# The state-space part of a decoder trunk: its two large matrices in quarters that share five small rooms

## The chip, the cores and the metric

The kernel runs on one core of a Trainium2 chip. The metric is the device time of one execution in microseconds (us). A core has five engines with an instruction queue each, worked off in order: TensorE (PE in the profile; its weight loads PEld), VectorE (DVE), ScalarE (ACT), GpSimd (POOL) and SyncE (SP), which here only issues DMAs. They meet through semaphores.

## The reference, cut to what matters

The program is a trunk of two residual layers on 512 tokens of width 1024 (an even layer, a routed expert block, an odd layer, a routed expert block). The change lies in the odd layer, whose mixer is attention (four heads; projections for keys, queries and values) beside a state-space layer "S5":

```python
def s5_mixer(u, ...):            # 32 groups of 16 channels, each one 64-dim complex diagonal state
    lam_bar = exp(lam * step)
    b_bar = ((lam_bar - 1) / lam) * b
    bu = einsum('gpc,btgc->btgp', b_bar, u)
    states = associative_scan(x_t = lam_bar * x_{t-1} + bu_t)
    y = einsum('gcp,btgp->btgc', c_mat, states).real + d_skip * u
    z = gelu(y)
    return z * sigmoid(z @ w_glu)
```

## The kernel before, in words

The 512 tokens of S5 are cut into 64 blocks of eight. Inside a block the output is one matrix product with the block's own inputs (a Toeplitz matrix, as the answer depends on the distance of two tokens alone); from block to block a state is carried by a scan. The generator `states()` does it in these steps:

- **Input map.** For two parts r (real, imaginary) and four quarters q of the groups, POOL and DVE build W, PE transposes it and ACT copies it into `Wt` (L1976 to L1990). `Wt` is one tile of 32x128 numbers on 128 partitions in the room `s5_wm`, which exists once.
- **Toeplitz kernel.** PE multiplies B by powers of the transition (`pk`, L2002), ACT copies the product to `Ks`, DVE adds the skip term, and POOL issues four DMAs of `Ks` to `Kd` in HBM (L2017).
- **States.** For two halves q of the groups PE computes `pj` from `Wt` and the inputs `U` (L2031); DVE and POOL rotate, scan and rotate back (L2037 to L2051) and leave the states in `XP`, first part r = 0, then r = 1.
- **Toeplitz form.** `M` (L2053) is again 32x128 numbers on 128 partitions and takes the same single room `s5_wm`. Eight DMAs (L2057) on SP's queue read `Kd` with overlapping rows.
- **Output.** For four quarters PE sums `M` times `U` (L2063) and Q times `XP` (L2067) in `pyy`, and ACT copies each quarter to z (L2070), which lies in the memory of the rotation's tables cs and sn (`s_csn`). Of these 48 matmuls of a quarter, 16 read `M`.

Beside `states()` runs `to_attention()`: projections (L1883 to L1885, three matmuls for each product, called `pu`) for keys, queries and values. Each takes its weights from a ring of three rooms that SP fills in the plan's order, in four pairs of 128 rows; ACT and DVE split a pair into `whi` (L160) and `wlo` (L161), and 24 matmuls use it. After keys and queries come a norm, rotary (`us`, `wk`: L1930, L1932, L1936) and transposes (`ptq`, L1941). `run_all` interleaves both generators step by step when the program is written; after that a scheduler in the compiler layer orders every engine's queue. The stage ends with the last `pu` of the values; attention and the GLU gate follow (`pzt`, L2203, is the first transpose of z). The weights of the GLU and of the output projection come over SP's queue behind those of `to_attention()`.

Of the kernel before, what the change touches and what calls it, by code (L numbers as in the profile page):

```python
# [8 lines left out]
F32 = mybir.dt.float32  # L9
# [3 lines left out]
AF = mybir.ActivationFunctionType  # L13
OP = mybir.AluOpType
# [1765 lines left out]
def odd_mixer(K, I, x, dbg):  # L1780
    tc, nc = K.tc, K.nc
    V, G, A = nc.vector, nc.gpsimd, nc.scalar
    ident = K.ident
    H = (slice(0, 64), slice(64, 128))
# [7 lines left out]
    def bank(name):  # L1792
        return ps.tile([128, 512], F32, name=name, tag="ps", bufs=4)
# [13 lines left out]
    Kd = dram.tile([32, 16, 240], F32, name="Kd")  # L1807
# [9 lines left out]
    for k in range(KD):  # L1817
        p = bank("pt")
# [145 lines left out]
    def flat_w(name, a, b):  # L1964
        return st.tile([128, 512], F32, name=name, tag="s5_w", bufs=4).rearrange("p (a b) -> p a b", a=a)

    def states():

        Bb = [S.B[:, r, :, None, :].to_broadcast([128, 16, 8, 16]) for r in range(2)]
        P7 = []  # L1970
        for r in range(2):
            p7 = st.tile([128, 16, 8], F32, name=f"s5_p7{r}", bufs=1)
            for s in range(8):
                G.tensor_copy(p7[:, :, s], S.L[:, r, :, 7 - s])
            P7.append(p7[:, :, :, None].to_broadcast([128, 16, 8, 16]))
        Wt = st.tile([128, 32, 128], F32, name="s5_Wt", tag="s5_wm", bufs=1)  # L1976
        Wt = Wt.rearrange("p (r i) n -> p r i n", r=2)
        for r in range(2):
            for q in range(4):
                sl = slice(4 * q, 4 * q + 4)  # L1980
                W = flat_w("s5_W", 4, 128).rearrange("p i (s c) -> p i s c", s=8)
                t8 = flat_w("s5_t8", 4, 128).rearrange("p i (s c) -> p i s c", s=8)
                G.tensor_tensor(W, Bb[0][:, sl], P7[r][:, sl], OP.mult)
                V.tensor_tensor(t8, Bb[1][:, sl], P7[1 - r][:, sl], OP.mult)
                V.tensor_tensor(W, W, t8, OP.add if r else OP.subtract)
                yield
                p = bank("pw").rearrange("p (a n) -> p a n", a=4)
                for a in range(4):
                    nc.tensor.transpose(p[:, a, :], W[:, a].rearrange("p s c -> p (s c)"), ident)
                A.activation(Wt[:, r, sl, :], p, AF.Copy)  # L1990

        Ks = st.tile([128, 2, 4, 128], F32, name="s5_Ks", tag="s5_xp", bufs=1)
        G.memset(Ks, 0.0)
        zt = st.tile([16, 112], F32, name="s5_zt", bufs=1)
        G.memset(zt, 0.0)
        G.dma_start(Kd.rearrange("g c n -> c g n")[:, :, 0:112], zt[:, None, :].to_broadcast([16, 32, 112]))
        for h in range(2):
            p = bank("pk").rearrange("p (a n) -> p a n", a=4)
            for i in range(16):
                a, cg = divmod(i, 4)  # L2000
                for r in range(2):
                    nc.tensor.matmul(p[32 * cg:32 * cg + 16, a, :], S.B[H[h], r, i, :],  # L2002
                                     S.Q[r][H[h], i, 0:8, :].rearrange("p j c -> p (j c)"),
                                     start=r == 0, stop=r == 1, tile_position=(64 * h, 32 * cg))
                if i == 7:
                    yield
            for cg in range(4):
                A.activation(Ks[32 * cg:32 * cg + 16, h], p[32 * cg:32 * cg + 16], AF.Copy)
            yield
        td = st.tile([128, 8, 16], F32, name="s5_td", bufs=1)  # L2010
        V.tensor_tensor(td, i16[:, None, :].to_broadcast([128, 8, 16]),
                        dsk[:, :, None].to_broadcast([128, 8, 16]), OP.mult)
        k0 = Ks.rearrange("p h a n -> p (h a) n")[:, :, 0:16]
        V.tensor_tensor(k0, k0, td, OP.add)
        for cg in range(4):
            dst = Kd.rearrange("(ha q) c n -> c ha q n", q=4)[:, :, cg, 112:240]
            G.dma_start(dst, Ks[32 * cg:32 * cg + 16].rearrange("p h a n -> p (h a) n"))  # L2017
        yield

        XP = st.tile([128, 2, 16, 65], F32, name="s5_XP", tag="s5_xp", bufs=1)  # L2020
        G.memset(XP[:, :, :, 0], 0.0)
        for q in range(2):
            X = [flat_w("s5_X", 8, 64) for r in range(2)]
            Y = [flat_w("s5_Y", 8, 64) for r in range(2)]
            pj = []
            for r in range(2):
                p = bank(f"pj{r}").rearrange("p (i k) -> p i k", i=8)
                for a in range(8):
                    i = 8 * q + a
                    for h in range(2):  # L2030
                        nc.tensor.matmul(p[H[h], a, :], Wt[:, r, i, 64 * h:64 * h + 64],  # L2031
                                         U[:, 16 * h + i, :], start=True, stop=True)
                pj.append(p)
                yield
            sl = slice(8 * q, 8 * q + 8)
            c, s = S.cs[:, sl], S.sn[:, sl]
            V.tensor_tensor(X[0], pj[0], c, OP.mult)  # L2037
            V.tensor_tensor(Y[0], pj[1], s, OP.mult)
            G.tensor_tensor(X[0], X[0], Y[0], OP.add)
            V.tensor_tensor(X[1], pj[1], c, OP.mult)  # L2040
            V.tensor_tensor(Y[1], pj[0], s, OP.mult)
            G.tensor_tensor(X[1], X[1], Y[1], OP.subtract)
            yield
            for r in range(2):
                V.tensor_tensor_scan(fl(Y[r]), fl(S.rho[:, sl]), fl(X[r]), 0.0, op0=OP.mult, op1=OP.add)
            yield
            X = [flat_w("s5_X", 8, 64) for r in range(2)]
            for r in range(2):
                V.tensor_tensor(X[0], Y[r], c, OP.mult)
                G.tensor_tensor(X[1], Y[1 - r], s, OP.mult)  # L2050
                V.tensor_tensor(XP[:, r, sl, 1:65], X[0], X[1], OP.add if r else OP.subtract)  # L2051
                yield
        M = st.tile([128, 32, 128], F32, name="s5_M", tag="s5_wm", bufs=1)  # L2053
        for s in range(8):
            src = bass.AP(tensor=Kd.tensor, offset=Kd.offset + (7 - s) * 16,
                          ap=[[240, 16], [3840, 32], [1, 128]])
            nc.sync.dma_start(M[16 * s:16 * s + 16], src)  # L2057
        for q in range(4):
            p = bank("pyy").rearrange("p (a n) -> p a n", a=4)
            for a in range(4):  # L2060
                i = 4 * q + a
                for h in range(2):
                    nc.tensor.matmul(p[H[h], a, :], U[:, 16 * h + i, :], M[:, 16 * h + i, :],  # L2063
                                     start=True, stop=False)
                for r in range(2):
                    for h in range(2):
                        nc.tensor.matmul(p[H[h], a, :], XP[H[h], r, i, 0:64],  # L2067
                                         S.Q[r][H[h], i, 1:9, :].rearrange("p j c -> p (j c)"),
                                         start=False, stop=r == 1)
            A.activation(z[:, :, 4 * q:4 * q + 4, :].rearrange("p t i c -> p i t c"),  # L2070
                         p.rearrange("p a (t c) -> p a t c", t=8), AF.Copy)
            yield
# [3 lines left out]
    st = tc.alloc_tile_pool(name="odd_st", bufs=1, side="right")  # L2076
    U = st.tile([128, 32, 64], F32, name="s5_U")
    todo = states()
    run_all((to_states(), 9), (part(todo, SN), SN))
    run_all((to_attention(), 30), (todo, 24))  # L2080
# [342 lines left out]
```

## Time and profile before

| | us |
|---|---|
| median of three runs | 1644.34 (1642.44 to 1648.06) |
| profiled execution, whole | 1643.12 |
| its span from first to last instruction | 1641.4 |
| PE busy in the span | 1528.8 (93%) |
| DVE, ACT, POOL busy | 819.5, 447.9, 230.4 |
| odd layer's projections and S5, first `pu` to first `pzt` | 872.30 to 1020.97 |

Times in the trace count from the span's start. In a timeline row, the first number is the start, the second the duration; a bracket is the idle time of the engine before it and what ended it. Matmuls overlap: one of 512 columns lasts 0.39 us at full clock, and the next starts 0.23 us after it.

### The profile page before, as it was taken

How to read it: one execution, taken by the hardware profiler on the slowest of the kernel's cores; microseconds unless marked ns; L12 is line 12 of the kernel's file. 1: busy time of each engine (PE TensorE's matmuls, PEld its weight loads, DVE VectorE, ACT ScalarE, POOL GpSimd, SP SyncE). 2: the span in 40 equal slices, each digit the busy share in tenths (PEclk: the TensorE clock that was granted, in tenths of full speed). 3: DMA queues.
4: the chain of work that ended last, by engine and by line, in shares of the span. 5: the costliest groups of instructions: out<-in, count | busy, mean ns of one | idle time of the engine just before them, and what ended most of it. 6: DMA issues, size and time to landing. Idle time of an engine off the chain costs nothing. (4 is left out here: it accounts for less than half of the span.)

```text
span 1641.4 us, 24906 instructions
## 1 busy us (share of the span) xinstructions
PE 1528.8 (93%) x9852; PEld 886.1 (54%) x9852; DVE 819.5 (50%) x1942; ACT 447.9 (27%) x1029; POOL 230.4 (14%) x268
## 2 busy tenths in 40 slices
PE   8998988999999999999998998799999999999997
PEld 6776666776444444433348775577544444433433
DVE  5577878776233333332764694764433333322323
ACT  5234434332212121111314533741021211211110
POOL 2342331200000000000211242501000000000000
PEclk9999999999999999999999999799999999999999
DMA  7210100177899999999992262209789999999996
GB/s 223 97 65 21 51 4 2 53 295 294 337 420 419 419 420 420 420 419 418 420 387 63 66 94 59 103 26 356 308 363 420 419 420 420 419 420 421 420 420 236
DMA packets 95564, 453.62 MB, mean 276 GB/s; under 512 B 12507, under 2 KB 30715, under 8 KB 49360
## 3 DMA queue, kind: packets, MB, share of 16 engines
q1 hardware_dynamic: 88144, 438.01, 67.9%
q0 software_dynamic: 5968, 13.58, 2.4%
q8 instruction: 80, 1.31, 0.3%
q10 hardware_dynamic: 1328, 0.36, 0.1%
q14 instruction: 44, 0.36, 0.1%
HBM read 452.91 MB, written 6.78 MB: 280 GB/s over the span
## 5 line engine op out<-in xcount | busy, mean ns | idle before, releaser
L1198 PE MATMUL pgu<-w,XT 128*64 128x512 f32 x1920 | 452.4, 596 | 22.3 <-DMA w<-in_moe_w_gate 19.1
L1198 PEld LDWEIGHTS pgu<-w,XT 128*64 128x64 f32 x1920 | 141.9, 137 | 312.3 <-issue 256.6
L1288 DVE TENSOR_TENSOR x<-pc,x 128x512 f32<-128x512 f32 x240 | 149.3, 682 | 163.6 <-PE pc L1198 163.6
L1198 PE MATMUL pd<-w,hTe 128*64 128x512 f32 x960 | 213.9, 598 | 0.6 <-ACT hTe L1336 0.6
L1327 DVE SCALAR_TENSOR_TENSOR hid<-hid,gs,pgu 128x512 f32<-128x512 f32 x32 | 23.9, 747 | 242.6 <-PE pgu L1198 234.9
L1095 POOL DMA_INDIRECT rows<-rows,idx x30 | 30.0, 999 | 759.6 <-DVE O L1215 590.3
L1198 PEld LDWEIGHTS pd<-w,hTe 128*64 128x64 f32 x960 | 66.6, 137 | 122.7 <-issue 112.9
L1256 ACT ACTIVATE XT<-pga,p_norm 128x128 f32<-128x128 f32 x240 | 68.3, 371 | 195.1 <-PE pga L1198 191.3
L1345 DVE TENSOR_TENSOR ylo<-pd,yhi 128x512 fp32r<-128x512 f32 (+1 forms) x68 | 44.8, 659 | 138.8 <-ACT yhi L1344 138.8
L1326 ACT ACTIVATE hid<-pgu,gs 128x512 f32<-128x512 f32 x32 | 22.0, 688 | 288.9 <-PE pgu L1198 288.9
L1198 PE MATMUL pc<-yhi,S 128*128 128x512 f32 x240 | 100.4, 418 | 0.0
L1198 PE MATMUL pc<-ylo,S 128*128 128x512 f32 x240 | 94.9, 395 | 0.0
L1344 ACT ACTIVATE yhi<-pd 128x512 fp32r<-128x512 f32 (+1 forms) x68 | 38.9, 572 | 170.9 <-PE pd L1198 153.4
L161 DVE SCALAR_TENSOR_TENSOR wlo<-w,p_norm,whi 128x512 fp32r<-128x512 f32 (+1 forms) x72 | 56.3, 813 | 44.9 <-ACT whi L160 44.9
L160 ACT ACTIVATE whi<-w,p_norm 128x512 fp32r<-128x512 f32 (+1 forms) x72 | 46.3, 692 | 77.8 <-PE pu L665 42.3
L1198 PEld LDWEIGHTS pc<-yhi,S 128*128 128x128 f32 x240 | 45.3, 189 | 34.1 <-issue 26.0
L664 PE MATMUL pu<-hhi,whi 128*128 128x512 f32 x144 | 58.6, 411 | 0.2 <-DVE u L672 0.2
L665 PE MATMUL pu<-hlo,whi 128*128 128x512 f32 x144 | 57.8, 401 | 0.0
L1884 PE MATMUL pu<-wlo,hhi 128*128 128x512 f32 x128 | 53.4, 419 | 3.4 <-DVE wlo L161 3.4
L666 PE MATMUL pu<-hhi,wlo 128*128 128x512 f32 x144 | 55.2, 402 | 0.0
L1883 PE MATMUL pu<-whi,hhi 128*128 128x512 f32 x128 | 51.0, 416 | 1.7 <-ACT us L1895 1.7
L1885 PE MATMUL pu<-whi,hlo 128*128 128x512 f32 x128 | 52.5, 416 | 0.0
(539 smaller groups left out, 2502.7 us busy)
## 6 DMA issues: line engine op xcount, KB each, us to landing
w<-in_moe_w_down SPq DMA_DIRECT2D x120, 1024.0 KB, 20.0
w<-in_moe_w_gate SPq DMA_DIRECT2D x120, 1024.0 KB, 20.0
w<-in_moe_w_up SPq DMA_DIRECT2D x120, 1024.0 KB, 20.2
w<-in_even_w_in SPq DMA_DIRECT2D x8, 1024.0 KB, 5.2
w<-in_moe_w_gate SPq DMA_DIRECT2D x16, 512.0 KB, 8.2
w<-in_moe_w_up SPq DMA_DIRECT2D x16, 512.0 KB, 9.6
w<-in_moe_w_down SPq DMA_DIRECT2D x16, 512.0 KB, 9.3
w<-in_odd_w_in SPq DMA_DIRECT2D x8, 1024.0 KB, 5.1
```

Source lines behind the costliest of these rows:

```text
L160: nc.scalar.activation(hi[:, k, :], w[:, k, :], AF.Copy, scale=g[:, k:k + 1])
L161: nc.vector.scalar_tensor_tensor(lo[:, k, :], w[:, k, :], g[:, k:k + 1], r32(hi[:, k, :]), op0=OP.mult, op1=OP.subtract)
L664: nc.tensor.matmul(out[j], a, hhi[:, kt, :], start=kt == 0, stop=False)
L665: nc.tensor.matmul(out[j], a, hlo[:, kt, :], start=False, stop=False)
L666: nc.tensor.matmul(out[j], b, hhi[:, kt, :], start=False, stop=kt == KD - 1)
L1198: return self.K.tc.keep_in_program_order(op(*args, **kw))
L1256: nc.scalar.activation(self.XTs[j][:, k, :], p[:, i, :], AF.Copy, scale=B.gain[:, k:k + 1])
L1288: V.tensor_tensor(self.x[:, t, c], p, self.x[:, t, c], OP.add)
L1345: self.nc.vector.tensor_tensor(yl[:, c], p, r32(yh[:, c]), OP.subtract)
L1883: nc.tensor.matmul(out[j], a, whi[:, k, :], start=kt == 0, stop=False)
L1884: nc.tensor.matmul(out[j], a, wlo[:, k, :], start=False, stop=False)
L1885: nc.tensor.matmul(out[j], b, whi[:, k, :], start=False, stop=kt == KD - 1)
```

## The change

`Wt` becomes four tiles of a quarter's size and `M` four others; all eight take turns in a room `s5_wm` that exists five times. The loop over Wt runs quarter by quarter. The fifth room is free from the start, so `M0` can be loaded as soon as `Kd` is written; M1 and M2 take the rooms of Wt0 and Wt1, which the first half of `pj` reads last, and M3 that of Wt2, which the second half reads last. `Ks` and `Kd` are laid out by quarters, so that a quarter of `M` is eight consecutive rows of groups. Each quarter is loaded by eight DMAs of 64 KB, where `M` was loaded by eight of 256 KB. The rooms take 20 KB of each partition, where they took 16 KB. The skip term is added in two operations of half the size.

```diff
-        Wt = st.tile([128, 32, 128], F32, name="s5_Wt", tag="s5_wm", bufs=1)
-        Wt = Wt.rearrange("p (r i) n -> p r i n", r=2)
-        for r in range(2):
-            for q in range(4):
+        Wt = [st.tile([128, 2, 4, 128], F32, name=f"s5_Wt{q}", tag="s5_wm", bufs=5) for q in range(4)]
+        for q in range(4):
+            for r in range(2):
...
-                A.activation(Wt[:, r, sl, :], p, AF.Copy)
+                A.activation(Wt[q][:, r], p, AF.Copy)
...
-        k0 = Ks.rearrange("p h a n -> p (h a) n")[:, :, 0:16]
-        V.tensor_tensor(k0, k0, td, OP.add)
+        for h in range(2):
+            k0 = Ks[:, :, h, 0:16]
+            V.tensor_tensor(k0, k0, td[:, 4 * h:4 * h + 4], OP.add)
...
+        M = []
+        def toeplitz(n):
+            for q in range(len(M), len(M) + n):
+                M.append(st.tile([128, 2, 4, 128], F32, name=f"s5_M{q}", tag="s5_wm", bufs=5))
+                for s in range(8):
+                    src = bass.AP(tensor=Kd.tensor, offset=Kd.offset + 8 * q * 3840 + (7 - s) * 16,
+                                  ap=[[240, 16], [3840, 8], [1, 128]])
+                    nc.sync.dma_start(M[q][16 * s:16 * s + 16].rearrange("p h a n -> p (h a) n"), src)
+        toeplitz(1)
...
         for q in range(2):
...
+            toeplitz(2 - q)
...
-        M = st.tile([128, 32, 128], F32, name="s5_M", tag="s5_wm", bufs=1)
-        for s in range(8):
-            src = bass.AP(tensor=Kd.tensor, offset=Kd.offset + (7 - s) * 16,
-                          ap=[[240, 16], [3840, 32], [1, 128]])
-            nc.sync.dma_start(M[16 * s:16 * s + 16], src)
...
-                    nc.tensor.matmul(p[H[h], a, :], U[:, 16 * h + i, :], M[:, 16 * h + i, :],
+                    nc.tensor.matmul(p[H[h], a, :], U[:, 16 * h + i, :], M[q][:, h, a, :],
```

The scheduler lays out the queues anew. In the rows below, lines of the changed kernel are 9 to 15 higher from the output on: its L2029 is the load of `M`, L2044 `pj`, L2072 and L2076 are the two products of `pyy`, L2079 is the copy to z.

On SP, the weights of S5 and of the projections, before:

```order
L1491 DMA w_8297<-in_odd_w_in 128x4x512
L1491 DMA w_8580<-in_s5_w_glu 128x4x512
L2057 DMA s5_M_8418<-Kd_7397 16x32x128 x8
L1491 DMA w_8642<-in_odd_w_out 128x2x1024
L1491 DMA w_8735<-in_odd_w_out 128x2x1024
```

and of the change (w_8297 and w_8328 are the second half of the values' weights):

```order
L1491 DMA w_8328<-in_odd_w_in 128x4x512
L2029 DMA s5_M0_8096<-Kd_7397 16x8x128 x8
L1491 DMA w_8611<-in_s5_w_glu 128x4x512
L2029 DMA s5_M1_8164<-Kd_7397 16x8x128 x8
L2029 DMA s5_M2_8173<-Kd_7397 16x8x128 x8
L2029 DMA s5_M3_8360<-Kd_7397 16x8x128 x8
L1491 DMA w_8673<-in_odd_w_out 128x2x1024
L1491 DMA w_8766<-in_odd_w_out 128x2x1024
```

The first quarter moved ahead of the GLU's weights, and the three others follow them.

On PE, at the first quarter of `pyy`, before (pu3_8579 is the last accumulator of the values in their second pair of weights, wlo_8613):

```order
L1884 MATMUL pu3_8579<-wlo_8613,hhi_7400 128x512
L1885 MATMUL pu3_8579<-whi_8612,hlo_7401 128x512
L2063 MATMUL pyy_8427<-s5_M_8418,s5_U_7525 64x128 x2
L2067 MATMUL pyy_8427<-s5_Q0_6601,s5_XP_8092 64x128 x2
L2067 MATMUL pyy_8427<-s5_Q1_6602,s5_XP_8092 64x128 x2
```

and of the change (pu3_8227 is the last accumulator of the queries, pu0_8607 the first of the values):

```order
L2044 MATMUL pj1_8311<-s5_U_7525,s5_Wt3_7581 64x64 x8
L1883 MATMUL pu3_8227<-whi_8375,hhi_7400 128x512
L1884 MATMUL pu3_8227<-wlo_8376,hhi_7400 128x512
L1885 MATMUL pu3_8227<-whi_8375,hlo_7401 128x512
L1883 MATMUL pu3_8227<-whi_8375,hhi_7400 128x512
L1884 MATMUL pu3_8227<-wlo_8376,hhi_7400 128x512
L1885 MATMUL pu3_8227<-whi_8375,hlo_7401 128x512
L2072 MATMUL pyy_8458<-s5_M0_8096,s5_U_7525 64x128 x2
L2076 MATMUL pyy_8458<-s5_Q0_6601,s5_XP_8105 64x128 x2
L1883 MATMUL pu0_8607<-whi_8613,hhi_7400 128x512
```

The first quarter's matmuls stand 45 products of the values further ahead, right behind the queries; 10 products of the values stand between its first four matmuls and the rest.

On ACT, around the first copy to z, before (whi_8612, whi_8644 and whi_8674 are the values' second, third and fourth pair):

```order
L160 ACTIVATE whi_8612<-w_8197,p_norm_84 128x512 x2
L1917 ACTIVATE sq_8385<-us3_8370 128x512
L160 ACTIVATE whi_8644<-w_8297,p_norm_84 128x512 x2
L2070 ACTIVATE s5_csn_6600<-pyy_8427 128x4x8x16
L160 ACTIVATE whi_8674<-w_8297,p_norm_84 128x512 x2
```

and of the change (whi_8643, whi_8675 and whi_8705 are the same three pairs):

```order
L160 ACTIVATE whi_8643<-w_8228,p_norm_84 128x512 x2
L1917 ACTIVATE sq_8425<-us3_8410 128x512
L2079 ACTIVATE s5_csn_6600<-pyy_8458 128x4x8x16
L160 ACTIVATE whi_8675<-w_8328,p_norm_84 128x512 x2
L160 ACTIVATE whi_8705<-w_8328,p_norm_84 128x512 x2
```

The copy to z moved ahead of the third pair's split. It overwrites the tables that DVE and POOL still read for the second half of the states (L2049 and L2050 of before), so it waits for those, and both splits wait behind it. On DVE, `wlo` of the third pair moved behind the last XP, and `wk` of the first token block ahead of `wlo` of the fourth pair.

## Rows read from the trace of the kernel before

**Rows 1.** Page, part 2: GB/s in 40 slices of the span.

```profile
GB/s 223 97 65 21 51 4 2 53 295 294 337 420 419 419 420 420 420 419 418 420 387 63 66 94 59 103 26 356 308 363 420 419 420 420 419 420 421 420 420 236
```

**Rows 2.** Tile s_M: duration ns min/median/max, first and last start; who waited; landing.

```profile
L2057 SPq DMA_DIRECT2D s_M<-Kd x8: 340/569/2412, 967.3 to 973.8; - x8
...
  PE pyy L2063: 4.4, 1
...
DMA to landing us min/median/max: 4.8/11.7/15.7
```

**Rows 3.** DMA view of 966 to 992 us: GB/s in 40 slices of 0.65 us.

```profile
GB/s 25 0 0 80 242 105 91 98 120 96 92 116 111 95 93 123 104 96 93 128 100 92 98 127 97 95 95 132 95 94 98 128 128 112 101 365 403 403 195 0
```

**Rows 4.** Timeline of PE around the load of M (start, us, engine, line, tiles).

```profile
965.13 2.08 PE L2031 MATMUL pj<-s_U,s_Wt 128*64 128x64 f32 x64
...
974.22 1.09 PE L1883 MATMUL pu<-whi,hhi 128*128 128x512 f32 x4
978.68 0.80 PE L1884 MATMUL pu<-wlo,hhi 128*128 128x512 f32 x1 [3.37 <-DVE wlo L161]
...
989.71 0.69 PE L2063 MATMUL pyy<-s_M,s_U 128*64 128x128 f32 x4 [4.37 <-issue]
...
995.50 0.51 PE L1883 MATMUL pu<-whi,hhi 128*128 128x512 f32 x1
...
1003.02 0.60 PE L1941 MATMUL ptq<-idt,wk 128*128 128x128 f32 x4
...
1016.43 0.48 PE L1883 MATMUL pu<-whi,hhi 128*128 128x512 f32 x1
...
1020.97 1.04 PE L2203 MATMUL pzt<-idt,s_csn 128*128 128x128 f32 x8
```

**Rows 5.** Stretches: PE, PEld, DVE, ACT, POOL busy (count), granted clock, DMA share, GB/s.

```profile
902.30:905.30 3.00, 3.00 (x8) 2.34 (x7) 2.34 (x1) 0.37 (x1) 3.00 (x9) 0.50 0.97 311
...
978.70:984.00 5.30, 5.30 (x13) 4.15 (x14) 5.20 (x10) 0.00 (x0) 1.75 (x2) 0.50 1.29 107
989.70:994.50 4.80, 4.79 (x36) 3.02 (x36) 4.62 (x6) 0.00 (x0) 3.22 (x2) 0.52 0.28 112
```

**Rows 6.** Timeline of PE: the idle time ahead of the first of these stretches.

```profile
900.99 0.50 PE L1883 MATMUL pu<-whi,hhi 128*128 128x512 f32 x1 [1.66 <-ACT us L1895]
```

**Rows 7.** Timeline of POOL: the stores of Kd, and the last product of the states.

```profile
943.85 2.14 POOL L2017 DMA_DIRECT2D Kd<-s_Ks  x4 [21.36 <-DVE rst L138]
...
983.52 1.84 POOL L2050 TENSOR_TENSOR s_X<-s_Y,s_csn 128x512 f32<-128x512 f32 x1 [1.14 <-DVE s_XP L2051]
```

**Rows 8.** DMA issues of 880 to 1010 us: KB each, median us to landing.

```profile
Kd<-s_Ks POOLq DMA_DIRECT2D x4, 64.0 KB, 2.5
```

**Rows 9.** Timeline of SP: the GLU's weights.

```profile
956.75 0.37 SPq L1491 DMA_DIRECT2D w<-in_s_w_glu  x1
```

**Rows 10.** Timeline of DVE: states, and the queries' rotary.

```profile
969.11 0.68 DVE L2051 TENSOR_TENSOR s_XP<-s_X 128x512 f32<-128x512 f32 x1
...
973.03 0.68 DVE L2051 TENSOR_TENSOR s_XP<-s_X 128x512 f32<-128x512 f32 x1
...
989.02 4.63 DVE L1930 TENSOR_TENSOR us<-us,rsq 128x512 f32<-128x512 f32 x4
993.57 0.75 DVE L1934 TENSOR_TENSOR sq<-us,ts 128x256 f32<-128x256 f32 x2
997.32 0.75 DVE L161 SCALAR_TENSOR_TENSOR wlo<-w,p_norm,whi 128x512 fp32r<-128x512 f32 x1 [3.00 <-ACT whi L160]
997.99 0.68 DVE L1936 TENSOR_TENSOR wk<-wk,sq 128x512 f32<-128x512 f32 x1
```

**Rows 11.** Timeline of ACT: the third pair's split, and the first copy to z.

```profile
974.42 1.34 ACT L160 ACTIVATE whi<-w,p_norm 128x512 fp32r<-128x512 f32 x2 [2.18 <-PE pu L1885]
995.67 0.60 ACT L2070 ACTIVATE s_csn<-pyy 128x512 f32<-128x512 f32 x1 [19.91 <-PE pyy L2067]
```

**Rows 12.** Waits of SP's queue, 1040 to 1160 us: total, times, longest.

```profile
SPq L1491 <- PE po L2251: 23.7, 1, 23.7
```

More of the change, by code (lines that the diff above doesn't have):

```diff
@@ L1989, in states @@
                     nc.tensor.transpose(p[:, a, :], W[:, a].rearrange("p s c -> p (s c)"), ident)
-                A.activation(Wt[:, r, sl, :], p, AF.Copy)
-        Ks = st.tile([128, 2, 4, 128], F32, name="s5_Ks", tag="s5_xp", bufs=1)
+                A.activation(Wt[q][:, r], p, AF.Copy)
+        Ks = st.tile([128, 4, 2, 128], F32, name="s5_Ks", tag="s5_xp", bufs=1)
         G.memset(Ks, 0.0)
@@ L2007, in states @@
             for cg in range(4):
-                A.activation(Ks[32 * cg:32 * cg + 16, h], p[32 * cg:32 * cg + 16], AF.Copy)
+                A.activation(Ks[32 * cg:32 * cg + 16, :, h], p[32 * cg:32 * cg + 16], AF.Copy)
             yield
@@ L2012, in states @@
                         dsk[:, :, None].to_broadcast([128, 8, 16]), OP.mult)
-        k0 = Ks.rearrange("p h a n -> p (h a) n")[:, :, 0:16]
-        V.tensor_tensor(k0, k0, td, OP.add)
+        for h in range(2):
+            k0 = Ks[:, :, h, 0:16]
+            V.tensor_tensor(k0, k0, td[:, 4 * h:4 * h + 4], OP.add)
         for cg in range(4):
             dst = Kd.rearrange("(ha q) c n -> c ha q n", q=4)[:, :, cg, 112:240]
-            G.dma_start(dst, Ks[32 * cg:32 * cg + 16].rearrange("p h a n -> p (h a) n"))
+            G.dma_start(dst, Ks[32 * cg:32 * cg + 16].rearrange("p a h n -> p (a h) n"))
         yield
+        M = []
[7 more added lines that the diff above has]
+        toeplitz(1)
         XP = st.tile([128, 2, 16, 65], F32, name="s5_XP", tag="s5_xp", bufs=1)
@@ L2030, in states @@
                     for h in range(2):
-                        nc.tensor.matmul(p[H[h], a, :], Wt[:, r, i, 64 * h:64 * h + 64],
+                        nc.tensor.matmul(p[H[h], a, :], Wt[i // 4][:, r, i % 4, 64 * h:64 * h + 64],
                                          U[:, 16 * h + i, :], start=True, stop=True)
```

## The prediction

> **What bounds the kernel now.** I read the page's GB/s line first. From about 1230 us (31st of 40 slices of 41 us) to the end the DMA engines move 420 GB/s in nearly every slice [rows 1]: there the stream of the experts' weights is the bound, so a change in the odd layer counts only if it makes that stream start earlier. The waits of SP's queue say that it does: SP stands 23.7 us for PE's output projection of the attention [rows 12]. That projection hangs on one chain from the odd layer's projections, on which PE is nearly always busy. So I carry a shift of the first `pzt` (1020.97, [rows 4]) one to one to the end.
>
> Next, PE's timeline around the load of `M`. PE stands 3.37 us for `wlo` at 978.68 and 4.37 us ahead of the first `pyy` at 989.71 [rows 4]; the tile view gives that second wait to `M` [rows 2]. After each, the table of stretches shows the lower clock level (1.2 GHz, 0.50 and 0.52) for 5.3 and 4.8 us [rows 5]. In the first, 13 matmuls start in 5.3 us, 0.41 each; at 2.4 GHz 20 of them start between 1016.43 and 1020.97, 0.227 each [rows 4]. A slow microsecond thus loses 1 - 0.227/0.41 = 0.45 us: 5.3 lose 2.4, 4.8 lose 2.1. The whole loss is 3.37 + 4.37 + 2.4 + 2.1 = 12.2 us.
>
> **The load of M.** `M` waits for the end of `pj` at 967.2 (965.13 + 2.08, [rows 4]); eight DMAs leave from 967.3 to 973.8 and land 4.8 to 15.7 us later [rows 2], the last near 989.5. Meanwhile the DMA engines move about 100 GB/s [rows 3], 0.26 MB each, 2.1 MB in all.
>
> After: POOL issues the stores of `Kd` from 943.85 for 2.14 us [rows 7], the last lands 2.5 us later [rows 8]: 948.5. Then `M0` goes out, 8 x 0.57 (the issue of [rows 2]) = 4.6 us, and its 0.52 MB take 5.2 us at 100 GB/s: it lands by 958. It stands ahead of the GLU's weights, which left at 956.75 [rows 9]; the eight issues end at 953, so they cost those nothing. M1 waits for the first half of `pj`, about 957, and M3 for the second, 967.2. The three have 1.57 MB, 15.7 us at 100 GB/s, and 1 MB of the GLU stands among them: all land by about 976. That is if 64 KB pieces flow as 256 KB pieces did; the rows of `Kd` read are as short as before. The added 24 issues are 24 x 0.57 = 13.7 us of SP's time, behind which only the output projection's weights stand, not urgent. The skip term's second operation adds some 0.3 us on DVE long before its reader: nothing.
>
> On such small pieces a rule speaks against the change. The row says that a 64 KB store takes 2.5 us from issue to landing [rows 8] and that eight loads fly at once [rows 2, 3]. The Trainium skill, "DMA: Bandwidth & Descriptors", section "Rules for kernel authors", says that many small transfers should be merged, since at such sizes most is overhead; its section "Anatomy of one DMA" gives about 2.0 us fixed plus bytes by 436 GB/s. One behind the other that is an estimate of 2.15 x 24 = 52 us for M1 to M3, and would cost PE about 5 us at the last quarter; overlapped it costs nothing. The next part goes by the rows; the serial case is a rival below.
>
> **What PE then waits for.** The order puts the first quarter's products 45 products of the values further ahead, so other waits come up.
>
> - `pj` ends 967.2, six `pu` follow to 968.6, M0's products, then PE needs XP of r = 0: 969.11 + 0.68 = 969.8 [rows 10]. Wait about 0.9. Ten `pu` (2.3) bring it to 972.5; XP of r = 1 is there at 973.03 + 0.68 = 973.7: wait about 1.2. The rest of the quarter I put at 3.1, an estimate: 36 records took 4.8 at 0.52 [rows 5], so about 4.8 x 0.52 = 2.5 at full clock, and 0.6 for records that the trace may lack: 976.8.
> - 14 `pu` (3.2) end near 980.2, 24 of the second pair (5.5) near 985.8. The 3.37 wait for `wlo` is gone, as that comes at 978.6 as before.
> - ACT's copy to z now stands ahead of the third pair's split, which ran at 974.42 before [rows 11]. It must wait for POOL's last product, 983.52 + 1.84 = 985.4 [rows 7]; copy 0.6, split 2 x 0.67: `whi` at 986.7 to 987.3, first `wlo` (0.75, [rows 10]) at 987.4. PE has used most of what it has by 985.8 and stands about 0.8. Its third pair then ends near 992.4, two `pu` more 992.9.
> - `us` starts at 989.02 as before, since DVE's earlier work is the same: 4.63 + 0.75 [rows 10] = 994.4, and `wk` 0.68: 995.0. Before, DVE stood 3.00 for `whi`, behind ACT's copy at 995.67 [rows 11], and `wk` came at 998.7. PE waits 995.0 - 993.0 = 2.0.
> - From the first `ptq` at 1003.02 to 1016.43 before took 13.41 [rows 4]. From 995.0 that gives 1008.4, and 22 `pu` (20 before) x 0.227 = 5.0: first `pzt` at 1013.4, against 1020.97, so 7.6 us earlier.
>
> From this goes what the new waits cost in clock. Their size (0.8 to 2.0 each, 4.9 in all) is below the two that go. The row nearest to them is the wait of 1.66 at 900.99 [rows 6]: it was followed by 0.50 for 3.0 us [rows 5], a loss of 1.35. I bound it by 0 (all are covered, and none shows) and 3 x 2.4 = 7.2 (each as after the 3.37). I take one such stretch, 1.35 to 1.6, between the two nearest rows, as part of it falls ahead of the wait for `wk`, which does not move with PE. Sum: 7.6 - 1.6 = 6.0 us gain. Around the span lie 1643.12 - 1641.4 = 1.7 us, unchanged: 1637.1 for the profiled execution, 1.2 under the median, so 1638.3 by the median. I say 1638.
>
> What could change it downstream: POOL's cast of the GLU's weights and the attention's first splits are shuffled by the scheduler too. I have no row of the new order; by the size of a copy and a split I allow 1.5 us either way.
>
> **The rivals.**
>
> 1. *The forecast:* two waits go, three small ones come, the gain of 4 to 8 us is carried to the end: 1636 to 1640.5. For it: SP's 23.7 [rows 12]; the XP, `us` and POOL times, which hang on none of the changed things. Chance 0.58.
>
> 2. *No new wait shows:* the whole 12.2 comes back: 1644.3 - 12.2 = 1632. For it: my times for `pu` assume full clock throughout; if PE comes later anyway, nothing waits. Against it: a PE that comes later has lost the same time elsewhere. Chance 0.08.
>
> 3. *The clock takes it back:* each of the three stands (2.1 around 970 to 974, 0.8 at 986, 2.0 at 993) is followed by 3.0 to 5.3 us at 0.50 [rows 5, 6], 1.35 to 2.4 each, 4.1 to 7.2 in all. Gain 7.6 - 5.6 = 2: about 1642. The same place is taken if the gain is lost downstream, in a copy or cast that comes late. For it: 1.66 was enough at 900.99. Against it: 0.8 is half of that. Chance 0.25.
>
> 4. *Slower: the 24 small DMAs fly one behind the other.* Each at 2.5 us [rows 8], from 957.2: M1 lands 977, M2 997, M3 1017. PE reaches the last quarter of `pyy` near 1003.7 (behind `ptq` at 995.0), waits 13.4 for M3, and 7.6 - 13.4 = -5.8: 1650. It decides from (1003.7 - 957.2)/24 = 1.9 us each. Against it: the eight loads before overlap, their engines at an even 100 GB/s [rows 3]. For it: no row shows loads of this size, and M1 and M2 reuse lanes on which eight others must have landed. Chance 0.09, that it does half of this included.
>
> **How the numbers follow.** A measurement of this kernel can tell about 0.3%, 4.9 us, from no change; faster means 1639.4 or less. Of the forecast's 0.58 some 0.44 lie below that, and rival 2 adds 0.08: faster 0.52. The rest of the forecast and nearly all of rival 3 are within 0.3%: 0.39. Rival 4 is slower: 0.09. The range runs from 1632 (rival 2) to 1646.5 (rival 3 with its upper bound and the small half of rival 4).
>
> **What would show it.** M0's eight loads start near 948.5 and land by 958; PE's first `pyy` starts near 969, not 990. M1 to M3 land by 976 to 980, and PE's idle time at `pyy` is put down to XP, not to `M`: otherwise rival 4. ACT shows a wait of some 9 us ahead of the first copy to z, ended by POOL or DVE, and the third pair's split behind it near 986. `wk` of the first token block comes near 995, the first `ptq` right behind it. The first `pzt` comes at 1013 to 1016. The gain of rival 3 would show as granted clock of 0.50 between 970 and 1000. Then SP's expert weights behind `po` leave about as much earlier as `pzt` did: 1104 rather than 1110. The forecast is wrong if `pzt` is early and that start is not, or if PE waits for `M` at all, or if the median is over 1641.

## The result, and the profile after

The changed kernel took 1636.01 us in the median of 8 runs (1634.69 to 1637.63), the kernel before 1642.43 (8 runs). The ratio is 0.9949, with a 95% interval of 0.9934 to 0.9963: some 6 to 11 us faster. (The 1644.34 from which the prediction starts was the median of the first three of those 8 runs.) The profiled execution took 1634.69, its span 1633.0 where it was 1641.4.

First, `M`. This is the view of the tile s_M, changed kernel: durations in ns, first and last issue, then issue to landing in us. Nobody is listed as waiting for it, where [rows 2] listed PE.

```profile
L2029 SPq DMA_DIRECT2D s_M<-Kd x32: 302/428/1707, 948.6 to 971.6; - x32
DMA to landing us min/median/max: 2.4/3.7/5.6
```

The last load is there by 971.6 + 5.6 = 977.2 at the latest; PE wants that quarter at 1004. SP's timeline has the order that was expected, M0 ahead of the GLU's weights, and then 24 loads in a row:

```profile
948.56 4.53 SPq L2029 DMA_DIRECT2D s_M<-Kd  x8
957.02 0.39 SPq L1491 DMA_DIRECT2D w<-in_s_w_glu  x1
957.51 14.57 SPq L2029 DMA_DIRECT2D s_M<-Kd  x24
```

Among the 24, SP stood 1.7 us at one load until the GLU's weights had landed, which `M` does not read (SP's waits: total, times, longest):

```profile
SPq L2029 <- DMA w<-in_s_w_glu: 1.7, 1, 1.7
```

PE's timeline (start, duration, in brackets the idle time ahead and who ended it) answers to [rows 4]. The waits of 3.37 and 4.37 are gone. Four short ones are new; a fourth quarter's matmul waits for nothing.

```profile
965.53 2.08 PE L2044 MATMUL pj<-s_U,s_Wt 128*64 128x64 f32 x64
...
969.13 0.44 PE L2072 MATMUL pyy<-s_M,s_U 128*64 128x128 f32 x4
970.10 0.44 PE L2076 MATMUL pyy<-s_Q,s_XP 64*64 64x128 f32 x4 [0.53 <-DVE s_XP L2065]
...
974.02 0.44 PE L2076 MATMUL pyy<-s_Q,s_XP 64*64 64x128 f32 x4 [0.95 <-DVE s_XP L2065]
...
986.88 0.96 PE L1883 MATMUL pu<-whi,hhi 128*128 128x512 f32 x3 [0.47 <-ACT whi L160]
...
995.33 0.63 PE L1941 MATMUL ptq<-idt,wk 128*128 128x128 f32 x4 [1.67 <-DVE wk L1936]
...
1013.97 1.03 PE L2212 MATMUL pzt<-idt,s_csn 128*128 128x128 f32 x8
```

ACT and DVE show whose these waits are. ACT's copy to z stood 13.12 us until POOL had read the tables, with both splits behind it [rows 11]; DVE's `us` started at the very time of [rows 10] and `wk` came at 994.49 + 0.69.

```profile
985.62 0.60 ACT L2079 ACTIVATE s_csn<-pyy 128x512 f32<-128x512 f32 x1 [13.12 <-POOL s_X L2064]
986.11 2.55 ACT L160 ACTIVATE whi<-w,p_norm 128x512 fp32r<-128x512 f32 x4
```
```profile
989.02 4.70 DVE L1930 TENSOR_TENSOR us<-us,rsq 128x512 f32<-128x512 f32 x4
...
994.49 0.69 DVE L1936 TENSOR_TENSOR wk<-wk,sq 128x512 f32<-128x512 f32 x1
```

The table of stretches from the end of the last `pj` to the first `pzt` adds it up (us; busy time of PE, PEld, DVE, ACT, POOL with counts; granted clock, DMA share, GB/s). Before:

```profile
967.21:1020.97 53.76, 46.02 (x312) 33.47 (x311) 32.69 (x53) 13.84 (x23) 13.55 (x10) 0.87 0.58 79
```

and after:

```profile
967.61:1013.97 46.36, 42.62 (x311) 30.09 (x311) 34.42 (x53) 14.28 (x24) 13.57 (x10) 1.00 0.21 60
```

The same work takes 7.40 us less: PE idles 53.76 - 46.02 = 7.74 before and 3.74 after (4.00 less), and is busy 3.40 less, as the clock is granted in full (1.00, [rows 5] had 0.50 twice).

The first `pzt` comes 7.00 us earlier, as the last `pj` ended 0.40 later. Behind `pzt` the gain wanders. SP's first expert load behind the output projection leaves 4.77 us earlier than [rows 12] led to (1110.16), the next group of four `w_up` loads 8.47 earlier, the end 8.4. Of the kernel before and of the changed one:

```profile
1110.16 0.33 SPq L1491 DMA_DIRECT2D w<-in_moe_w_gate  x1
...
1198.00 4.24 SPq L1491 DMA_DIRECT2D w<-in_moe_w_up  x4
```
```profile
1105.39 0.33 SPq L1491 DMA_DIRECT2D w<-in_moe_w_gate  x1
...
1189.53 4.29 SPq L1491 DMA_DIRECT2D w<-in_moe_w_up  x4
```

The granted clock says where. Both kernels have stretches at half clock in the attention, in part at other places; at the router and at the experts' gather only the kernel before has them. These are the two stretches as a whole, from `pzt` to the first expert load and from there to the `w_up` loads, before and after:

```profile
1020.97:1110.16 89.19, 75.56 (x393) 54.11 (x391) 59.01 (x139) 51.92 (x165) 25.96 (x16) 0.89 0.17 60
1110.16:1198.00 87.84, 81.08 (x406) 56.80 (x408) 37.35 (x164) 14.98 (x38) 8.73 (x11) 0.94 0.85 329
```
```profile
1013.97:1105.39 91.42, 76.86 (x393) 55.01 (x391) 59.63 (x139) 51.37 (x164) 25.96 (x16) 0.87 0.17 58
1105.39:1189.53 84.14, 76.92 (x406) 54.99 (x408) 37.36 (x164) 14.98 (x38) 8.73 (x11) 1.00 0.88 341
```

In the second, PE is busy 4.16 us less at full clock for the same 406 matmuls, and idle 0.46 more: that is the whole 3.70 by which it is shorter. Single places, again before and after (one in the attention, the router, the gather):

```profile
1062.00:1071.00 9.00, 5.12 (x31) 3.13 (x33) 6.84 (x22) 3.85 (x14) 0.00 (x0) 0.97 0.14 56
1147.00:1152.00 5.00, 3.98 (x12) 1.46 (x12) 4.54 (x24) 0.00 (x0) 1.27 (x2) 0.66 1.00 392
1188.00:1196.00 8.00, 6.53 (x28) 3.99 (x30) 3.33 (x15) 3.25 (x10) 0.88 (x1) 0.57 0.64 257
```
```profile
1062.00:1070.00 8.00, 6.50 (x22) 3.67 (x22) 5.91 (x22) 5.85 (x23) 0.00 (x0) 0.57 0.00 0
1140.00:1150.00 10.00, 7.92 (x53) 4.08 (x52) 8.10 (x40) 1.13 (x3) 1.80 (x3) 1.00 0.99 384
1180.00:1190.00 10.00, 6.97 (x44) 3.40 (x42) 3.35 (x15) 5.13 (x12) 1.01 (x1) 1.00 0.70 245
```

### The profile page after: what moved, and what is told of

It is laid out like the page before. It is cut to its first block, busy times and chain, and to the rows that moved or that the text cites. A ratio compares the mean times of both kernels' runs of the same rounds, so it can differ in the third digit from the quotient of the medians.

```text
span 1633.0 us, 24946 instructions
## 1 busy us (share of the span) xinstructions
PE 1522.4 (93%) x9852; PEld 880.8 (54%) x9852; DVE 821.6 (50%) x1943; ACT 447.5 (27%) x1029; POOL 230.9 (14%) x268
## 5 line engine op out<-in xcount | busy, mean ns | idle before, releaser
L1345 DVE TENSOR_TENSOR ylo<-pd,yhi 128x512 fp32r<-128x512 f32 (+1 forms) x68 | 44.8, 660 | 137.5 <-ACT yhi L1344 137.5
```

What stands on the lines that cost most here:

```text
L1345: self.nc.vector.tensor_tensor(yl[:, c], p, r32(yh[:, c]), OP.subtract)
```

## The experiments

Three marks are read from every trace: A, end of the last `pj` to the first `pzt` (PE's timeline); B, from there to the first expert load behind the output projection; C, from there to the first group of four `w_up` loads (both SP's timeline). The ratio is to runs of the kernel before that were taken beside each.

| trace | A | B | C | half clock within A | granted clock in B, in C | ratio to before (95%) |
|---|---|---|---|---|---|---|
| before | 53.76 | 89.19 | 87.84 | 977 to 984, 987 to 995 | 0.89, 0.94 | 1 |
| before_again | 55.87 | 90.21 | 86.19 | 987 to 998 | 0.87, 0.96 | 0.9993 (0.998 to 1.0006) |
| changed | 46.36 | 91.42 | 84.14 | none | 0.87, 1.00 | 0.9949 (0.9934 to 0.9963) |
| changed_again | 46.39 | 91.49 | 84.17 | none | 0.87, 1.00 | 0.9957 (0.9944 to 0.9971) |
| four_rooms | 46.37 | 91.63 | 83.72 | none | 0.85, 1.00 | 0.9953 (0.9935 to 0.9972) |
| loads_doubled | 46.37 | 91.37 | 84.05 | none | 0.87, 1.00 | 0.9951 (0.9938 to 0.9964) |
| quarters_late | 46.39 | 91.46 | 84.05 | none | 0.85, 1.00 | 0.9954 (0.9939 to 0.997) |
| quarters_late_2 | 47.15 | 89.16 | 87.74 | 974 to 982 | 0.90, 0.94 | one run |
| halves_late | 47.23 | 89.08 | 87.69 | 976 to 983 | 0.90, 0.94 | 0.995 (0.993 to 0.997) |
| outputs_last | 49.95 | 89.69 | 85.89 | none | 0.89, 0.96 | 0.9972 (0.996 to 0.9984) |
| block_by_block | 44.77 | 91.16 | 87.69 | none | 0.87, 0.94 | 0.9956 (0.9941 to 0.9971) |
| block_by_block_2 | 44.78 | 90.96 | 86.29 | none | 0.85, 0.96 | one run |
| late_block_by_block | 47.28 | 89.34 | 84.91 | 979 to 986 | 0.92, 0.98 | 0.9948 (0.9931 to 0.9966) |
| late_block_2 | 44.79 | 90.15 | 88.08 | none | 0.87, 0.94 | one run |

C goes with the clock granted in it: 83.7 to 84.2 us in the five traces with 1.00, 84.9 at 0.98, 85.9 to 86.3 at 0.96, 87.7 to 88.1 at 0.94. B does so loosely: 89.1 to 89.7 at 0.89 to 0.92, 90.1 to 91.6 at 0.85 to 0.87.

### Does it repeat?

The changed kernel, unaltered:

> The changed kernel once more, unaltered, for a second trace. Theory: the first pzt comes 7.0 us earlier than before in every execution, since it hangs on waits that repeat (0.5 and 0.95 for XP, 0.5 for whi, 1.7 for wk), and the end varies around that by up to 3 us, as the stretches at half clock further down (in the attention and at the routed experts' gather) fall on other instructions: ratio 0.994 to 0.997. Rival: the 8.4 us by which the span became shorter repeats as it is, with the same stretches at half clock: 0.9949 within 0.0005, and a granted clock near 0.69 about 50 us behind pzt again.

A is the same to 0.03 us, B and C to 0.07; from there to the end it took 446.5 us where the first trace took 443.5. So the half clock in the attention (1062 to 1070; here 1061 to 1068) stands at the same place of the program in both executions. The spread arises in the experts' stream, and also ahead of the stage: the last `pj` ended at 965.73 here, 1.88 earlier than in the first trace. Neither text is wholly right: A and the clock pattern repeat, the end does not.

> The kernel before once more, unaltered, for a second trace: the first pzt 55.8 us behind the start of the last pj, with the waits of 3.4 for wlo and 4.4 for M and a stretch at half clock behind each. Theory (the half-clock stretches follow the program's own pattern of work and idle time): they stand at the same places as in the first trace, also those at the router (1147) and at the experts' gather (1188), which the traces of the changed kernel lack. Rival (they fall differently in every execution): one or more of the four stand elsewhere or are gone, and the stretch from the first expert load to the end differs by 2 us or more from the first trace's 531.

Neither pattern held: the stretch at 977 to 984 was gone, those at the router and the gather were there (1151 and 1192 here, the second shorter). And this trace corrects the reading of the kernel before:

```profile
978.92 0.50 PE L1884 MATMUL pu<-wlo,hhi 128*128 128x512 f32 x1 [3.36 <-DVE wlo L161]
...
991.22 0.69 PE L2063 MATMUL pyy<-s_M,s_U 128*64 128x128 f32 x4 [8.06 <-issue]
```

Behind the same wait for `wlo` PE kept the full clock here, came to `pyy` earlier, and waited 8.06 instead of 4.37 for `M`. When `pyy` started was set by when M landed (by the tile views at most 974.3 + 16.8 = 991.1 here, 973.8 + 15.7 = 989.5 in the first trace), not by how PE spent the time until then.

### Is it the early room, the fifth room, or the waiting by quarters?

One room as before, all loads behind the last `pj`, but in quarters (`Wt` and `M` are one tile each in the one room, and PE's order is close to that of before):

```diff
-        toeplitz(1)
...
-            toeplitz(2 - q)
...
+        Mt = st.tile([128, 4, 2, 4, 128], F32, name="s5_M", tag="s5_wm", bufs=1)
+        toeplitz(4)
         for q in range(4):
             p = bank("pyy").rearrange("p (a n) -> p a n", a=4)
```

> One room as before: the input map is one tile and M one tile, and all 32 loads of 64 KB wait for the last pj (967), but PE waits for one quarter at a time. PE's order is that of before, but for the first quarter, which stands 11 products of the values earlier. Theory S (it is enough to wait for a quarter at a time, the early room adds little): the first eight loads are there by 975, PE gets to pyy near 983 and waits for nothing; the 4.4 wait and the slow stretch behind it (2.1) go, the 3.4 wait for wlo stays, first pzt near 1014.5 and 1636 to 1638. Theory E (the early room is what counts): 32 issues of 0.43 and 2.1 MB at 100 GB/s end as late as before, the last quarters keep PE waiting, and less than 2 us is gained: 1641 to 1643.

Theory S, with A 46.39 where its 1014.5 makes 47.3 (1014.5 - 967.2). The tile view, and PE's timeline:

```profile
L2030 SPq DMA_DIRECT2D s_M<-Kd x32: 339/429/437, 969.2 to 983.8; - x32
DMA to landing us min/median/max: 2.3/2.9/3.1
```
```profile
980.50 0.50 PE L1884 MATMUL pu<-wlo,hhi 128*128 128x512 f32 x1 [3.23 <-DVE wlo L161]
...
982.10 0.44 PE L2072 MATMUL pyy<-s_M,s_U 128*64 128x128 f32 x4
...
996.92 0.49 PE L1884 MATMUL pu<-wlo,hhi 128*128 128x512 f32 x1 [1.21 <-DVE wlo L161]
```

PE still waits 3.23 for `wlo`, but not for `M`, and ends the stage as early as the changed kernel. Within the intervals the whole gain is there without an early room. Smaller loads alone would not do it: the last one is there by 983.8 + 3.1 = 986.9 at the latest, so a PE that waits for all of `M` at 982.10 would stand up to 4.8 us (an estimate; that kernel was not run).

> As with the quarters loaded late into one room, but in two halves: sixteen loads of 128 KB, of which PE waits for eight. Theory S: the first half (1.05 MB at 100 GB/s) is there near 978, PE gets to it near 982, the second near 989, wanted at 1003: first pzt as early as with quarters (48.5 us behind the start of the last pj, before 55.8), 1636 to 1638. Rival: the first half lands later than PE comes (full DMA engines, landing 11 us as the 256 KB loads did): PE waits 2 to 3 us and only part of the gain is left, 1638 to 1640.

The edit against quarters_late (the loads alone; the helper that goes and the list of the quarters are left out):

```diff
-        toeplitz(4)
+        for f in range(2):
+            for s in range(8):
+                src = bass.AP(tensor=Kd.tensor, offset=Kd.offset + 16 * f * 3840 + (7 - s) * 16,
+                              ap=[[240, 16], [3840, 16], [1, 128]])
+                nc.sync.dma_start(Mt[16 * s:16 * s + 16, 2 * f:2 * f + 2].rearrange("p q h a n -> p (q h a) n"), src)
```

```profile
L2059 SPq DMA_DIRECT2D s_M<-Kd x16: 302/392/528, 966.0 to 978.6; - x16
DMA to landing us min/median/max: 3.5/9.5/10.3
```
```profile
977.32 0.80 PE L1884 MATMUL pu<-wlo,hhi 128*128 128x512 f32 x1 [3.23 <-DVE wlo L161]
...
980.60 0.70 PE L2066 MATMUL pyy<-s_M,s_U 128*64 128x128 f32 x4
```

Two pieces do as well as four by the time (0.995), and PE does not wait for `M`. A is 0.8 longer than in quarters_late, with half clock at the wait for `wlo` this time. From the start of the last `pj` it is 49.3, where 48.5 was expected (in quarters_late 48.47).

> The changed kernel with four rooms, not five: the first quarter of M waits for the first half of pj as the second does, and its loads stand behind the GLU's weights; the other engines' orders are the same. Theory: M0 goes out at 957.4, lands by 963 to 966 in spite of the GLU's 1 MB, before PE wants it at 969.1; nothing changes: the changed kernel's time within 1 us. Rival (the fifth room is needed): the GLU's megabyte and M1 push M0 beyond 969, PE waits 1 to 4 us there and the second quarters are late for nobody: 1 to 4 us slower than the changed kernel.

```diff
-                M.append(st.tile([128, 2, 4, 128], F32, name=f"s5_M{q}", tag="s5_wm", bufs=5))
+                M.append(st.tile([128, 2, 4, 128], F32, name=f"s5_M{q}", tag="s5_wm", bufs=4))
```

(and so for Wt). The theory: A 46.37, PE's waits 0.53, 0.95, 0.49 and 1.71 as in the changed kernel. The fifth room, and 4 KB of each partition, buy nothing.

### Are the loads hidden?

```diff
-                for s in range(8):
+                for s in 2 * list(range(8)):
```

> The changed kernel with every load of M's quarters issued twice (64 loads of 64 KB, all the same data; the scheduler puts the GLU's weights behind them, the other engines' orders are the same). Theory (the loads are hidden with some 28 us to spare): 64 issues of 0.43 end near 980, M3 is there by 985 and wanted at 1004, the GLU's weights are there by 985 and wanted at 1014: no change, 1635 to 1637.5. Rival (64 KB loads go one behind the other at some 2 us each): M3 lands after 1050 and PE waits more than 40 us: 1680.

No change, with twice the loads. Issue to landing stays short, so they overlap; SP takes 31.86 us for 64 issues, 0.50 each.

```profile
947.40 31.86 SPq L2029 DMA_DIRECT2D s_M<-Kd  x64
```
```profile
DMA to landing us min/median/max: 2.4/2.6/3.4
```

### Could the order alone do it?

The kernel before with `M` in one piece; one empty step ahead of the output part lets the scheduler put all of `pyy` behind the values:

```diff
+        for _ in range(1):
+            yield
         for q in range(4):
             p = bank("pyy").rearrange("p (a n) -> p a n", a=4)
```

> The kernel before, M in one piece and loaded as before, but with one empty step ahead of the output part when the program is written; the scheduler then puts all of pyy behind the values' products (102 pu, then ptq and the four quarters), and the attention's first scores ahead of pzt. Theory O (what cost the time was that PE came to the first quarter before M was there, whatever the reason): no wait for M, none of the slow stretch behind it, and about 4 to 6 us are gained by the time of the first expert load (1105 to 1106 in the first trace's time): 1637 to 1639. Rival (z then comes too late for the GLU and attention behind it): PE waits in the attention instead, and nothing is gained or lost: 1642 to 1645.

Both in part: 0.9972 (0.996 to 0.9984), about 4.6 us, over half of the gain from the order alone. The wait of 3.37 for `wlo` stays, a second one of 1.49 comes, and z comes late, as the rival had it, if for less:

```profile
992.81 0.50 PE L1884 MATMUL pu<-wlo,hhi 128*128 128x512 f32 x1 [1.49 <-DVE wlo L161]
1015.02 1.18 PE L2205 MATMUL pzt<-idt,s_csn 128*128 128x128 f32 x8 [1.35 <-ACT s_csn L2193]
1018.69 0.49 PE L2108 MATMUL psc<-qkT,qkT 64*128 64x128 f32 x4 [2.49 <-ACT pe L2117]
```

### What bounds the stage now?

The changed kernel; the queries' norm of each token block is issued behind `wk` of the block before:

```diff
-            V.tensor_tensor(q3, q3, rs[:, t, :, None].to_broadcast([128, 8, 64]), OP.mult)
+            norm = lambda: V.tensor_tensor(q3, q3, rs[:, t, :, None].to_broadcast([128, 8, 64]), OP.mult)
+            if i == 0 and t:
+                with tc.issue_after(wk[-1]):
+                    norm()
+            else:
+                norm()
```

(`wk` keeps the sums' instructions.)

> The changed kernel, with the queries' norm, rotary products and sum (DVE) done one token block after the other instead of all four norms first. PE's order: the first ptq stands five products earlier. Theory (in the changed kernel PE's last wait, 1.67 us at 995.3, is set by DVE's chain to wk alone, so the time that M and the rooms gave back ends there): first wk near 992.6, the wait below 0.8, first pzt 1.6 us earlier (near 1012.4), and the end about as much earlier: 1634.5. Rival: DVE waits for POOL's products between the blocks, the values' last wlo come later and PE waits for those: no change, 1636, or worse.

A fell by 1.6 as the theory had it, and the wait for `wk` is gone: in PE's timeline the first `ptq` has no bracket. DVE's first `wk` is done 24.8 us behind the last `pj` (964.16), in the changed kernel 27.6.

```profile
983.42 0.97 PE L1883 MATMUL pu<-whi,hhi 128*128 128x512 f32 x3 [0.48 <-ACT whi L160]
989.09 0.63 PE L1947 MATMUL ptq<-idt,wk 128*128 128x128 f32 x4
```
```profile
988.25 0.69 DVE L1942 TENSOR_TENSOR wk<-wk,sq 128x512 f32<-128x512 f32 x1
```

So DVE's chain set the end of A in the changed kernel. The time did not follow (0.9956): C is 87.69 where the changed kernel has 84.14, with half clock at the router and the gather:

```profile
1138.00:1142.00 4.00, 4.00 (x11) 1.43 (x12) 3.73 (x19) 0.00 (x0) 0.83 (x1) 0.57 0.99 388
1179.00:1186.00 7.00, 6.57 (x30) 3.60 (x30) 2.61 (x14) 3.27 (x10) 1.01 (x1) 0.51 0.64 265
```

> Quarters loaded late into one room (as in quarters_late), with the queries' norm, products and sum one token block after the other (as in block_by_block). From the end of the last pj to the first pzt the traces so far show 53.8 and 55.9 (before), 46.4 (changed, and quarters_late), 44.8 (changed with blocks). Theory (once PE waits by quarters, DVE's chain to wk sets the end of the stage, and the early rooms buy nothing even where that chain is shorter): 44.8 within 0.5, and 1635 to 1637. Rival (the early rooms show their worth as soon as DVE is out of the way, since only then does PE come to the waits for wlo and M that the early first quarter covers): 46 or more.

The rival's number came, 47.28, and its reason in part: the wait of 3.24 for `wlo` that it named is there, but PE waits for nothing behind it; half clock at 979 to 986 (0.52) makes the difference. The next three runs ask whether that belongs to the program.

> late_block_by_block once more. Theory as above: 44.8 if the slow stretch at 979 to 986 is gone this time, 47.3 if not. Rival (each program has its own pattern): 47.3 and the slow stretch again.

> quarters_late once more, for a second trace. Its first trace showed full clock behind PE's wait of 3.2 for wlo, and 46.4 from the last pj to the first pzt; halves_late and late_block_by_block, with the same wait, showed half clock for some 7 us behind it, and 47.2. Theory (whether the half clock follows that wait differs from execution to execution, and what the early first quarter buys is to be rid of it): either 46.4 without a slow stretch at 977 to 987 or about 47.2 with one, in any of the three. Rival (each program has its own pattern): 46.4 and no slow stretch again.

> block_by_block once more. Both theories: 44.8 from the last pj to the first pzt, as PE has no long wait there. On the slow stretches at 1138 and 1179: theory, gone or elsewhere in this execution; rival, there again, and the stretch from the first pzt to the experts' fourth pair of loads is 178.9 again, where it was 175.4 to 175.7 in the traces of the changed kernel.

The late kernels went by the theory: 44.79 without a slow stretch, 47.15 with one. Of block_by_block the slow stretches stood at the router and the gather again (the second shorter, B + C 177.3, not 178.9): between the two texts. The same wait and its neighbourhood, in two executions of one kernel, late_block_by_block and late_block_2:

```profile
979.00:986.00 7.00, 5.92 (x30) 3.78 (x30) 6.90 (x13) 0.00 (x0) 2.36 (x2) 0.52 1.07 136
```
```profile
976.00:986.00 10.00, 6.98 (x61) 4.79 (x62) 9.84 (x13) 0.23 (x1) 4.34 (x4) 1.00 0.70 162
```

## Why the prediction was right, and where not

- **The forecast held, in part by luck.** 1638 was predicted, 1636.0 measured; a gain of 6.0 against 6.4 by the medians of 8 runs (8.4 by the ratio: 0.0051 x 1642.4). The other cases did not come: not 1632, not 1642, not 1650. In the profiled executions the span is 8.4 shorter: 7.40 in A and 1.47 in B and C, less 0.40 by which the last `pj` ended later. The sum took off 1.6 that were not lost (see the clock term) and had nothing for B and C.
- **The loads, right.** M0 left at 948.56 (forecast 948.5), all is there by 977.2 (976). Rival 4 is refuted by the changed kernel itself and by loads_doubled; of the landings that it feared to wait for, SP's waits show 1.7 us in all for one that `M` does not need. The Trainium skill, "DMA: Bandwidth & Descriptors", section "Rules for kernel authors", would have many small transfers merged into a large one, as under 64 KB most is overhead. These pieces lie at that edge, and here the trace shows no loss by them: 2.1 MB in 64 KB pieces were all there 17.7 us after the first issue (quarters_late, 983.8 + 3.1 - 969.2, at most), in 256 KB pieces after some 22 [rows 2, 3]. The 2.0 us that the prediction took from the Trainium skill, "DMA: Bandwidth & Descriptors", section "Anatomy of one DMA", are given there for DMAs that GpSimd issues. These are SP's, and they overlap: 64 left in 31.86 us, each landing 2.6 us after its issue in the median (loads_doubled).
- **The new waits, right in place, somewhat too long.** 0.9, 1.2, 0.8 and 2.0 were forecast; 0.53, 0.95, 0.47 and 1.67 came. `pzt` was put at 1013.4 and came at 1013.97.
- **The clock term, wrong.** 1.6 us were taken off for half clock behind the new waits. No trace with the early first quarter has any within A. The row used, 3.0 us at 0.50 behind a wait of 1.66, is a stretch and not a price per wait.
- **"I carry a shift of the first `pzt` one to one to the end", wrong by the step.** `pzt` came 7.0 earlier, the first expert load 4.8: B grew by 2.2 and C shrank by 3.7 us, with the clock granted in them (0.89 to 0.87, 0.94 to 1.00). In the table B + C lies between 174.3 and 178.9 over 14 traces, so a single trace tells little of what a gain in A becomes.
- **"The whole loss is 12.2 us", wrong.** Three of its four terms (3.37, 2.4 and 4.37) stand one behind the other ahead of one event, the landing of `M`, and don't add up. before_again has the 3.36 without the slow stretch and 8.06 instead of 4.37. The forecast did not rest on this sum (it went forward from DVE's times), but rival 2 did.
- **The cause, named only in part.** The prediction followed M0 through the early room. quarters_late shows that the wait by quarters gives the time, and halves_late that two pieces do. The early first quarter also rids PE of the 3.2 for `wlo`. While DVE's chain ends the stage that is worth 0.0 to 0.9 of A (46.36 to 46.39 against 46.39, 47.15, 47.23); with that chain shorter, 0.0 or 2.5 (44.8 against 44.79 and 47.28).

That DVE's chain ends the stage is shown for the changed kernel by block_by_block. Why the half clock falls on the router and the gather in some traces and not in others stays open. The length of the stage does not decide it: the kernel before (A 53.76) and block_by_block (44.77) have it there, the changed kernel (46.36) has not; nor does the program alone, as quarters_late has none there and quarters_late_2 has.

## What to carry to other kernels

If an engine waits for one large load into a shared room, let it wait for a part of the load first: here one room, 16 loads and no early start gave as much as eight small rooms. Waits and slow stretches ahead of one late event are not to be added; go forward from what the next event hangs on. A gain in one stage is read from marks in several traces, as the clock behind it can take back or add as much as the gain of a second edit.

## What the runs showed of the hardware

The same wait of PE, 3.2 to 3.4 us for `wlo`, stands in eight traces. In four of them (before, quarters_late_2, halves_late, late_block_by_block) the clock falls to half while PE stands in that wait (in before, 0.62 at 977 to 978) and stays there for some 7 us, in four (before_again, quarters_late, late_block_2, outputs_last) it does not; the kernel before, quarters_late and the kernel of late_block_by_block show both, each in two executions of one program. The Trainium skill, "TensorE: Matmul & The Clock Gate", section "Part 1: The HAM clock gate", says that what watches PE for this runs freely and does not start anew with a kernel, so that the point of change varies between runs. These pairs agree with that; no run here shows the watch itself.

Smaller loads of the same rows landed sooner each, too: 2.9 us in the median at 64 KB (quarters_late), 9.5 at 128 KB (halves_late), 11.7 at 256 KB [rows 2]. As a whole only those of 64 KB were quicker: at most 17.7 us from the first issue to the last landing, against 22.9 (978.6 + 10.3 - 966.0) at 128 KB. The DMA view has the engines busy 0.4 to 0.8 of the time with the 64 KB loads, and 0.9 or more with the others; why stays open.
